# Attention operands padded to 128 rows of zeros, masks in fp32r of 256 columns, one transfer for both heads, and other banks and places for sums, loads and projection steps

## The chip, the cores and the metric

One core of one Trainium2 chip runs the whole kernel. The metric is the device time of an execution in microseconds; the time before is the median of three runs, 1707.32 us (1706.2 to 1708.44).

## The reference

One step of a hybrid layer on two sequences: a prompt of 1024 frames, and a sample of 64 new frames with 256 frames of cache. Each layer normalises the input, makes one combined projection, feeds a part of its columns to RWKV-7 heads and a part to attention heads with a forget bias, projects both results back, and ends in a SwiGLU feed-forward. The part that the change touches is the attention with the output projection behind it (8 heads of 64):

```python
def _fox_attend(q, k, v, lc_q, lc_k, pos_q, pos_k):
    s = jnp.einsum('bqhd,bshd->bhqs', q, k, preferred_element_type=jnp.float32) * (HEAD_DIM ** -0.5)
    decay_bias = jnp.transpose(lc_q, (0, 2, 1))[..., :, None] - jnp.transpose(lc_k, (0, 2, 1))[..., None, :]
    causal = pos_k[None, :] <= pos_q[:, None]
    p = jax.nn.softmax(jnp.where(causal, s + decay_bias, -jnp.inf), axis=-1)
    return jnp.einsum('bhqs,bshd->bqhd', p.astype(v.dtype), v)
...
    mix = jnp.concatenate([y_rwkv, y_fox], axis=-1) @ w_out
    x = x + gt1[:, None] * mix
    h2 = _rms_norm(x, norm2_g) * (1 + sc2[:, None]) + sh2[:, None]
    ffn = (jax.nn.silu(h2 @ w_ffn_gate) * (h2 @ w_ffn_up)) @ w_ffn_down
```

## The kernel before, in words

The 1088 tokens go in two halves: half 0 is the first 512 prompt tokens, half 1 the other 512 and the 64 of the sample. In the profiled execution the projections and the RWKV heads take about the first 660 us, with the first attention pair of half 0 among their end. From about 680 to 909 us runs the attention of the rest, together with the output projection of half 0; from there to 1702 us the output projection of half 1 and the feed-forward.

**Attention.** Heads go in pairs, four pairs for each half. Numbers are split into a high and a low part (both in fp32r, a format of TensorE), and a score is the sum of two matmuls into one bank of PSUM (`pst`): `ka` with `qa` (128 rows: high and low keys against the high queries twice) and `kb` with `qb`. `kb` and `qb` have 73 rows: 64 of high keys or low queries, five rows of ones against the row maxima, and four rows of the summed log-forget values. Before the scores, `att_max` makes a maximum of each query's scores from `kb` and `qc` alone (bank `pmx`, reduced by VectorE into `nmx`); `att_rows` transposes the maxima on TensorE (`pnm`) and VectorE writes them into the five rows of `qb`. `att_main` then runs over blocks of 128 keys: score, mask on the diagonal, exponential on ScalarE (`pt`), sum over blocks on VectorE and GpSimd (`acc`), and the product with the values two blocks later (`pav`). A pair ends with the column sums over `acc` (`psm`), their inverse by Ln and Exp on ScalarE, and the scaled result `fy`. In half 1, the 64 sample queries have their own scores and values (`pss`, `pvs`).

**Masks** are matmuls too: the identity times `cmask`, 128 columns of bf16, added to the bank of the diagonal block.

**Loads.** The operands lie in DRAM as `qx` and `kx`, 132 rows for each head. `pair_load` fetches them, in parts: 0 is `qc` and `kb`, 1 is `qb`, `qa` and `ka`, 2 the values. Each head has its own tiles and transfers, 8 in part 0 and 10 in part 1. All are issued by SyncE (SP) in program order, beside the stores.

**Order.** The Tile scheduler orders the first part. In `att_second` the order of TensorE is that of the program (`te.on`): the four pairs of half 1 ("big" pairs) are walked block by block, and at each of 25 yields of a big pair one step is taken of `low`, the generator of pairs 1 to 3 of half 0 ("low" pairs). When these have ended, `load_mix` fetches the mixed rows, and two blocks later `proj_steps` begins, the output projection of half 0 (`po`, 64 steps of three matmuls), with three steps at a block. The low pairs keep their operands in rows of the buffers of the mix (`mixrh`, `mixrl`, `mixfh`, `mixfl`) and their `pt` and `acc` in the residual buffer (`x_0`).

**Banks.** `pmx` has two banks ("mx"), which it shares with `pnm`, `psm`, `pss` and `pvs`; `pst` has three ("st"), and the low pairs' `pav` and `po` lie in "mm".

Of the kernel before, what the change touches and what calls it, by code (L numbers as in the profile page):

```python
# [64 lines left out]
class K:  # L65
# [631 lines left out]
    def ones_rows(self):  # L697
        nc = self.nc

        cones = self.slot([2, 448], F32R, name="cones")  # L700
        nc.vector.tensor_copy(cones, self.ones[0:2, 0:1].to_broadcast([2, 448]))
        for scr, r, n, w in ((self.qx, 130, SP + SS, 272), (self.kx, 128, SP + PAST + SS, 448)):
            for i in range(0, n, w):
                nc.sync.dma_start(scr[:, r:r + 2, i:i + w].rearrange("h r t -> r h t"),
                                  cones.bitcast(F32)[:, 0:w].unsqueeze(1).to_broadcast([2, 8, w]))

    def logf(self, hf):
# [70 lines left out]
        for g in (order[0:4], order[4:]):  # L778
            if not g:
                continue  # L780
            g = sorted(g, key=lambda e: e[2])
            if g[0][2] != hf.t0:
                pr = self.ps([32, 4, P], tag="fx", name="plr")
                rows = self.slot([32, 4, P], F32R, name="lrow", tag="fx")
            ck = g[0][2]
            prf, rf = pr.rearrange("r x t -> r (x t)"), rows.rearrange("r x t -> r (x t)")
            for i, _, c, m, _ in g:
                nc.tensor.transpose(prf[:, c - ck:c - ck + m], q4[0:m, i].rearrange("p a h -> p (a h)"),
                                    self.ident[0:m, 0:m])
            w = sum(m for _, _, _, m, _ in g)  # L790
            nc.vector.tensor_copy(rf[:, 0:w], prf[:, 0:w])
            cq = g[0][4]
            wq = sum(m for _, _, _, m, c in g if c is not None)
            for part in range(2):
                r = 16 + 8 * part
                nc.sync.dma_start(self.kx[:, 130 + part, ck:ck + w], rf[r:r + 8, 0:w].bitcast(F32))
                nc.sync.dma_start(self.qx[:, 128 + part, cq:cq + wq], rf[8 * part:8 * part + 8, 0:wq].bitcast(F32))
# [38 lines left out]
    def put_split(self, src, j, t0, n, is_k):  # L836

        nc = self.nc
        hi = self.slot([P, 576], F32R, name="shi", tag="fx")
        lo = src.bitcast(F32R)  # L840
        self.split(hi[:, 0:n], lo, src, pool_lo=self.pool_lo)
        for x, r in ((hi, 0 if is_k else 64), (lo, 64 if is_k else 0)):
            for h in range(2):
                t = (self.kx if is_k else self.qx)[2 * j + h, r:r + 64]
                nc.sync.dma_start(t[:, t0:t0 + n], x[64 * h:64 * h + 64, 0:n].bitcast(F32))
# [24 lines left out]
    def att_consts(self, ap):  # L870
        nc = self.nc
        self.identb = ap.tile([P, P], BF16, name="identb")
        nc.vector.tensor_copy(self.identb, self.ident)
        self.cmask = []
        for x in range(2):
            cm = self.slot([P, P], name="cm")
            nc.gpsimd.memset(cm, 0.0)
            nc.gpsimd.affine_select(out=cm, in_=cm, compare_op=ALU.is_ge, fill=NEG, base=0,
                                    pattern=[[2 * x - 1, P]], channel_multiplier=1 - 2 * x)
            self.cmask.append(ap.tile([P, P], BF16, name=f"cmask{x}"))  # L880
            nc.vector.tensor_copy(self.cmask[x], cm)
# [4 lines left out]
    def ones_keys(self, kb):  # L886
        self.nc.gpsimd.tensor_copy(kb[64:69], self.ones[64:69, 0:1].to_broadcast([5, kb.shape[1]]))

    def no_rows(self, qc):
        self.nc.gpsimd.memset(qc[64:69].bitcast(F32), 0.0)  # L890

    def pair_ops(self, pool):

        nq, nk = 640, SP + PAST + SS
        t = {n: pool.tile(s, F32 if n == "v" else F32R, name=n)
             for n, s in (("kb2", [73, nk]), ("kb3", [73, nk]), ("v", [P, 11, P]), ("qb0", [73, nq]), ("qb1", [73, nq]),
                          ("qa0", [P, 576]), ("qa1", [P, 576]), ("ka0", [P, nk]), ("ka1", [P, nk]),
                          ("kb0", [73, nk]), ("kb1", [73, nk]), ("qc0", [73, nq]), ("qc1", [73, nq]))}
        self.pops = {n: [t[f"{n}{i}"] for i in range(4 if n == "kb" else 2)] for n in ("kb", "qc", "ka", "qa", "qb")}
        self.pops["v"] = t["v"]  # L900
        for t in self.pops["kb"]:
            self.ones_keys(t)
        for t in self.pops["qc"]:
            self.no_rows(t)
            self.nc.gpsimd.memset(t[:, 576:640].bitcast(F32), 0.0)

    def pair_bufs(self, g, big):
# [3 lines left out]
        g["tags"] = {"st": "st", "mx": "mx", "pv": "pv" if big else "mm", "sm": "mx"}  # L911
        return g

    def pair_get(self, j):

        g = {n: [t[(2 * j + h) % len(t)] for h in range(2)] for n, t in self.pops.items() if n != "v"}
        g["v"] = self.pops["v"]
        return self.pair_bufs(g, True)

    def pair_first(self, pool):  # L920

        g = {n: [pool.tile([r, 512], F32R, name=f"{n}f{h}") for h in range(2)]
             for n, r in (("kb", 73), ("qc", 73), ("ka", P), ("qa", P), ("qb", 73))}
        for h in range(2):
            self.ones_keys(g["kb"][h])
            self.no_rows(g["qc"][h])
        return self.pair_bufs(g, True)

    def pairs_low(self):

        (m0, m1), (l0, l1) = self.mixhi, self.mixlo
        a, b, c, d, e, f = [[t[:, k, 0:512] for k in range(4)] for t in (m0.a, l0.a, m1.a, l1.a, m0.b, l0.b)]
        one = {"kb": a[0:2], "qc": a[2:4], "ka": b[0:2], "qa": b[2:4], "qb": c[0:2]}
        two = {"kb": c[2:4], "qc": d[0:2], "ka": d[2:4], "qa": [e[2], f[2]], "qb": [e[3], f[3]]}
# [6 lines left out]
        for j in (1, 2, 3):  # L941
            g = out[j]
            for k in ("kb", "qc", "qb"):
                g[k] = [t[0:73] for t in g[k]]
            if j < 3:
                for h in range(2):
                    self.ones_keys(g["kb"][h])
                    self.no_rows(g["qc"][h])
# [5 lines left out]
    def pair_load(self, j, hf, g, part):  # L954
# [5 lines left out]
        for h in range(2):  # L960
            hd = 2 * j + h
            ka, kb, qa, qb, qc = [g[x][h] for x in ("ka", "kb", "qa", "qb", "qc")]
            if part == 0:
                ld(qc[0:64, 0:n], self.qx[hd, 64:128, q])
                ld(qc[69:73, 0:n], self.qx[hd, 128:132, q])
                ld(kb[0:64, 0:NK], self.kx[hd, 0:64, 0:NK])
                ld(kb[69:73, 0:NK], self.kx[hd, 128:132, 0:NK])
            elif part == 1:
                ld(qb[0:64, 0:n], self.qx[hd, 0:64, q])
                ld(qb[69:73, 0:n], self.qx[hd, 128:132, q])  # L970
                for r in (0, 64):
                    ld(qa[r:r + 64, 0:n], self.qx[hd, 64:128, q])
                ld(ka[:, 0:NK], self.kx[hd, 0:128, 0:NK])
# [9 lines left out]
    def att_max(self, j, hf, g):  # L983
# [4 lines left out]
        for h in range(2):  # L988
            pc = self.tpool.tile([P, 4, 2], F32, tag="pc", name="pc") if hf.smp else None
            for t in range(5 if hf.smp else 4):  # L990
                smp = t == 4
                qn, nk, k0 = (SS, 320, SP) if smp else (P, hf.t0 + (t + 1) * P, 0)
                for x, c in enumerate(range(0, nk, 512)):
# [5 lines left out]
                    if c + m == nk:  # L999
                        d = 0 if smp else m - qn  # L1000
                        te.matmul(ps[0:qn, d:d + qn], self.identb[0:qn, 0:qn], self.cmask[0][0:qn, 0:qn], start=False,
                                  stop=True, skip_group_check=True)
# [6 lines left out]
    def att_rows(self, j, hf, g):  # L1009
# [5 lines left out]
        for h in range(2):  # L1015
            r = slice(32 * h, 32 * h + 5)
            nc.vector.tensor_tensor(g["qb"][h][64:69, 0:nt * P].rearrange("p (t q) -> p t q", q=P),
# [3 lines left out]
    def att_main(self, j, hf, g):  # L1021
# [11 lines left out]
        def scores(b, c0):  # L1033
            r = []
            for h in two:
# [6 lines left out]
                if diag:  # L1042
                    te.matmul(ps[:, c0:c0 + P], self.identb, self.cmask[1], start=False, stop=True, skip_group_check=True)
# [42 lines left out]
        if hf.smp:  # L1086
            ps = self.ps([P, 2, 3, SS], tag=tags["sm"], name="pss")
            for h in two:
# [4 lines left out]
                te.matmul(ps[0:SS, h, 2], self.identb[0:SS, 0:SS], self.cmask[1][0:SS, 0:SS], start=False, stop=True,  # L1093
# [28 lines left out]
        pd = self.ps([P, 512], tag=tags["sm"], name="psm")  # L1122
# [33 lines left out]
    def proj_steps(self, hf):  # L1156

        w = [self.load_w(self.A["w_out"][0], [P, KT, P])]
        for o in range(KT):
# [5 lines left out]
            for k in range(KT):  # L1165
                for y, (l, r) in enumerate(((wh, mh), (wh, ml), (wl, mh))):
                    self.te.matmul(ps[:, 0:hf.n], l[:, k], r[:, k, 0:hf.n], start=(k == 0 and y == 0),
                                   stop=(k == KT - 1 and y == 2))
                if k == KT - 1:
# [3 lines left out]
    def att_second(self, hf, h0, g, low):  # L1173
# [3 lines left out]
        po, mix, start = iter(()), iter(()), 0  # L1177
        for j in range(4):
# [4 lines left out]
            for b in self.att_main(j, hf, g):  # L1183
                if low and next(low, 1) == 1:
                    low, mix = None, self.load_mix(h0)
                    fill(mix, 2)
                    self.residual_x(h0)
                    start = 8 * j + (b if isinstance(b, int) else 7) + 2
                if b == "v":
                    if nxt:  # L1190
# [3 lines left out]
                        fill(po, 2)  # L1194
                        self.att_rows(j + 1, hf, nxt)
                    fill(po, 2)
                elif b in ("h", "b"):
                    fill(mx, 1)
                    fill(mix, 1)
                else:  # L1200
                    if start and 8 * j + b == start:
                        po = self.proj_steps(h0)
                    fill(po, 3)
                    fill(mx, b % 2)
                if b == 7 and nxt:
                    fill(mx, 99)
                    self.pair_load(j + 1, hf, nxt, 1)
                    fill(po, 1)
            fill(po, 1)
# [7 lines left out]
    def load_mix(self, hf):  # L1217
# [3 lines left out]
        for m in range(4 if hf.smp else 5):  # L1221
# [361 lines left out]
    def run(self):  # L1583
        tc, nc, A, O = self.tc, self.nc, self.A, self.O
        halves = [Half(0), Half(1)]
        with ExitStack() as top:
# [8 lines left out]
            self.qx = D1("qx", [8, 132, SP + SS])  # L1595
# [117 lines left out]
            mix1, x1s, attp, mix0 = [top.enter_context(ExitStack()) for _ in range(4)]  # L1713
# [4 lines left out]
            self.pair_ops(L(attp, "attp"))  # L1718
# [5 lines left out]
            gs = self.pairs_low()  # L1724
            g = self.pair_get(0)
# [16 lines left out]
            attp.close()  # L1742
# [214 lines left out]
```

## Time and profile before

| | |
|---|---|
| median of three runs | 1707.32 us |
| profiled execution | 1703.8 us, its span 1702.1 us |
| instructions | 31944, of them 12783 matmuls |
| TensorE busy | 1635.9 us, 96% of the span |
| TensorE idle | 66.2 us (the span less its busy time) |
| mean granted clock of TensorE | 0.969 of full speed |
| VectorE, ScalarE, GpSimd busy | 1050.2, 660.6 and 180.0 us |
| DMA | 200.18 MB, mean 118 GB/s |

The profiled execution's time is its span and 1.7 us around it, and it lies 3.5 us under the median of the runs. A matmul's busy time has its length at the clock that was granted: at a clock of 0.50 TensorE can be busy all the time and do half the work. So the table's 96% has to be read with the granted clock of the stage beside it.

### The profile page before, as it was taken

To read this page: it belongs to the slowest core of one execution; us is meant where nothing else is said; L and a number is where in the kernel's file an instruction comes from. 1 tells how busy PE (TensorE), PEld (TensorE's weight loads), DVE (VectorE), ACT (ScalarE), POOL (GpSimd) and SP (SyncE) were. 2 spreads that over 40 slices of the span, in tenths; PEclk is the share of its full clock that TensorE was granted. 3 is DMA by queue.
4 is the path that set the end of the run, shared out by engine and by line. 5 is a ranking of instruction groups with operands and counts; after the bars stand their busy time and mean duration, and the time that the engine had idled before them with its cause. 6 is when DMAs were issued, how large, how long until landed. Compare 5 with 4: busy or idle time off the path is not lost.

```text
span 1702.1 us, 31944 instructions
## 1 busy us (share of the span) xinstructions
PE 1635.9 (96%) x12783; PEld 1400.2 (82%) x12783; DVE 1050.2 (62%) x2162; ACT 660.6 (39%) x1284; POOL 180.0 (11%) x314
## 2 busy tenths in 40 slices
PE   6999999999999998699999999999999999999999
PEld 3767767788878886455668999999999999999998
DVE  6677676758767635454556985555555555545545
ACT  4544465745454354033335643333333333112210
POOL 1101101120202204132341000000000000000000
PEclk8999999999999999587999999999999999999999
DMA  8544466512233344824644433222222215423313
GB/s 308 162 112 119 140 190 201 157 52 64 58 96 79 95 126 122 211 72 115 187 146 152 152 116 103 80 77 76 77 77 77 76 65 161 154 94 96 96 38 124
DMA packets 130019, 200.18 MB, mean 118 GB/s; under 512 B 61838, under 2 KB 68526, under 8 KB 129870
## 3 DMA queue, kind: packets, MB, share of 16 engines
q1 hardware_dynamic: 129870, 198.14, 38.5%
q8 instruction: 100, 1.64, 0.4%
q14 instruction: 49, 0.40, 0.1%
HBM read 154.90 MB, written 43.19 MB: 116 GB/s over the span
## 4 chain that ended last, share of the span: by engine, by line
PE 78%; DVE 8%; ACT 4%; DMA 4%; issue 2%; SPq 2%; POOL 0%; DVEq 0%; ACTq 0%; POOLq 0%
PE pd L1515 15%; PE pfe L1400 8%; PE pfc L1400 8%; PE pfa L1400 7%; PE pmm L323 4%; PE pmm L325 4%; PE pmm L324 4%; PE pfb L1400 4%; PE pst L1860 3%; PE pbs L404 2%; PE po L1860 2%; PE pav L1860 2%; PE pmx L1860 1%; PE pS L662 1%; SPq L958 1%
## 5 line engine op out<-in xcount | busy, mean ns | idle before, releaser
L323 PE MATMUL pmm<-hhi,whi 128*128 128x288 f32 (+1 forms) x624 | 218.0, 350 | 2.4 <-ACT pb L346 2.4
L324 PE MATMUL pmm<-hlo,whi 128*128 128x288 f32 (+1 forms) x624 | 216.0, 346 | 0.2 <-DVE hlo L301 0.2
L325 PE MATMUL pmm<-hhi,wlo 128*128 128x288 f32 (+1 forms) x624 | 213.1, 342 | 0.0
L241 ACT CAST whi<-wraw 128x1024 fp32r<-128x1024 f32 (+2 forms) x116 | 99.2, 855 | 222.8 <-PE pd L1515 163.4
L1515 PE MATMUL pd<-al,whi 128*128 128x512 f32 (+1 forms) x528 | 172.4, 327 | 0.0
L1515 PE MATMUL pd<-ah,whi 128*128 128x512 f32 (+1 forms) x528 | 172.2, 326 | 0.0
L1515 PE MATMUL pd<-ah,wlo 128*128 128x512 f32 (+1 forms) x528 | 172.2, 326 | 0.0
L1519 DVE SCALAR_TENSOR_TENSOR x1t<-pd,mod,x1t 128x512 f32<-128x512 f32 x192 | 91.1, 498 | 106.8 <-PE pd L1515 106.2
L323 PEld LDWEIGHTS pmm<-hhi,whi 128*128 128x128 f32 x624 | 118.6, 190 | 17.8 <-issue 3.7
L324 PEld LDWEIGHTS pmm<-hlo,whi 128*128 128x128 f32 x624 | 118.5, 190 | 11.2 <-issue 1.7
L325 PEld LDWEIGHTS pmm<-hhi,wlo 128*128 128x128 f32 x624 | 118.3, 190 | 10.9 <-issue 1.7
L245 DVE TENSOR_TENSOR wlo<-wraw,whi 128x1024 fp32r<-128x1024 f32 (+2 forms) x108 | 104.7, 970 | 28.0 <-ACT whi L241 27.7
L1515 PEld LDWEIGHTS pd<-ah,whi 128*128 128x128 f32 x528 | 99.1, 188 | 7.1
L1515 PEld LDWEIGHTS pd<-ah,wlo 128*128 128x128 f32 x528 | 99.1, 188 | 7.1
L1515 PEld LDWEIGHTS pd<-al,whi 128*128 128x128 f32 x528 | 99.1, 188 | 7.0
L1400 PE MATMUL pfc<-hh,hS 128*128 128x256 f32 (+1 forms) x352 | 102.3, 291 | 1.1 <-ACT hh L1302 1.1
L1400 PE MATMUL pfc<-hh,lS 128*128 128x256 f32 (+1 forms) x352 | 102.4, 291 | 0.0
L1400 PE MATMUL pfa<-hh,whi 128*128 128x256 f32 (+1 forms) x352 | 102.1, 290 | 0.0
L1400 PE MATMUL pfa<-hl,whi 128*128 128x256 f32 (+1 forms) x352 | 101.8, 289 | 0.0
L1400 PE MATMUL pfa<-hh,wlo 128*128 128x256 f32 (+1 forms) x352 | 101.6, 289 | 0.0
L1400 PE MATMUL pfc<-hl,hS 128*128 128x256 f32 (+1 forms) x352 | 101.3, 288 | 0.0
L1347 ACT CAST hS<-wraw 128x512 fp32r<-128x512 f32 x88 | 53.6, 619 | 62.3 <-PE pfc L1400 61.4
(437 smaller groups left out, 4106.4 us busy)
## 6 DMA issues: line engine op xcount, KB each, us to landing
wraw<-in_w_in_dram SPq DMA_DIRECT2D x52, 512.0 KB
wada<-in_w_ada_dram SPq DMA_DIRECT2D x48, 512.0 KB
as<-actscr SPq DMA_DIRECT2D x22, 544.0 KB
wraw<-in_w_gate_dram SPq DMA_DIRECT2D x22, 512.0 KB
wraw<-in_w_up_dram SPq DMA_DIRECT2D x22, 512.0 KB
wraw<-in_w_down_dram SPq DMA_DIRECT2D x40, 256.0 KB
wraw<-in_w_out_dram SPq DMA_DIRECT2D x16, 512.0 KB
actscr<-sg SPq DMA_DIRECT2D x22, 288.0 KB
```

The source lines that it names most:

```text
L241: nc.scalar.copy(hi, src)
L245: eng.tensor_tensor(lo, src, hi.bitcast(F32), op=ALU.subtract)
L323: nc.tensor.matmul(ps[0:M, 0:n], whi[:, k, 0:M], xhi[:, k, off:off + n], start=(k == 0), stop=False)
L324: nc.tensor.matmul(ps[0:M, 0:n], whi[:, k, 0:M], xlo[:, k, off:off + n], start=False, stop=False)
L325: nc.tensor.matmul(ps[0:M, 0:n], wlo[:, k, 0:M], xhi[:, k, off:off + n], start=False, stop=(k == kt - 1))
L404: nc.tensor.matmul(ps[:, 0:n], w, x[:, off:off + n], start=True, stop=True)
L662: nc.tensor.matmul(ps, kb[:, c], sv[:, c], start=True, stop=True)
L1347: nc.scalar.copy(w[x][0], src)
L1400: nc.tensor.matmul(ps, l[:, k], r[:, s, k], start=(first and k == 0 and y == 0), stop=(k == 3 and y == 2), skip_group_check=True)
L1515: nc.tensor.matmul(ps[:, 0:n], w[:, i], x[:, t:t + n], start=(i == 0 and y == 0), stop=(i == len(fs) - 1 and y == 2))
L1519: nc.vector.scalar_tensor_tensor(dst, ps[:, so - off:so - off + l], self.mod[:, 40 + o, b:b + 1], dst, op0=ALU.mult, op1=ALU.add)
L1860: return self.pin(self.tc.nc.tensor.matmul(*a, **k))
```

## The change

The change has these parts.

1. **Rows.** All tiles of `kb`, `qc` and `qb` get 128 rows. GpSimd clears rows 64 to 127 and writes the ones at 96 to 100 (`aux_rows`); the four log-forget rows move from 69 to 64. The matmuls of these operands then have 128 rows instead of 73.
2. **Masks.** The identity and `cmask` are fp32r, and a mask has 256 columns, of which 128 are zeros (64 columns at the sample's scores).
3. **Transfers.** A tile holds both heads, `[128, 2, n]`, and one transfer fills it: part 0 has 2 transfers, part 1 has 4, in the order `qa`, `qa`, `ka`, `qb`. `qx` gets 136 rows and `kx` another order, so that the 68 rows of an operand lie together; writing the log-forget rows of `qx` takes four more transfers for the ones.
4. **Buffers.** `kb` of the big pairs is double (`kb0`, `kb1`), all else single. `pair_ops` stands behind `pairs_low`, so its clearing follows that of the low pairs.
5. **Banks.** `psm` has a tag of its own, "dn": banks of "st" for the big pairs; the low pairs' `psm`, `pnm` lie in "mm".
6. **Steps beside the big pairs.** `side()` takes 30 low steps for a big pair instead of 25 (four at "v"), and the projection's steps begin as soon as the low pairs have ended, with 2 or 3 at a block.
7. **Rows of the mix.** The projection adds rows 4 to 7 first; `load_mix` begins with row 4, and this one is fetched at the start of the second half.

The core of the diff:

```diff
     def att_consts(self, ap):
...
-            self.cmask.append(ap.tile([P, P], BF16, name=f"cmask{x}"))
-            nc.vector.tensor_copy(self.cmask[x], cm)
+            self.cmask.append(ap.tile([P, 3 * P], F32R, name=f"cmask{x}"))
+            nc.gpsimd.memset(self.cmask[x].bitcast(F32), 0.0)
+            nc.vector.tensor_copy(self.cmask[x][:, P:2 * P], cm)
...
-    def ones_keys(self, kb):
-        self.nc.gpsimd.tensor_copy(kb[64:69], self.ones[64:69, 0:1].to_broadcast([5, kb.shape[1]]))
-
-    def no_rows(self, qc):
-        self.nc.gpsimd.memset(qc[64:69].bitcast(F32), 0.0)
+    def aux_rows(self, kb, *rest):
+        nc = self.nc
+        for t in (kb, *rest):
+            nc.gpsimd.memset(t[64:128].bitcast(F32), 0.0)
+        nc.gpsimd.tensor_copy(kb[96:101], self.ones[96:101, 0:1].unsqueeze(2).to_broadcast([5, *kb.shape[1:]]))
...
+        t = {n: pool.tile([P, *s], F32 if n == "v" else F32R, name=n)
+             for n, s in (("kb1", [2, nk]), ("v", [11, P]), ("qb", [2, nq]), ("qa", [2, 576]), ("ka", [2, nk]),
+                          ("kb0", [2, nk]), ("qc", [2, nq]))}
+        self.pops = t
+        self.aux_rows(t["kb0"], t["qc"], t["qb"])
+        self.aux_rows(t["kb1"])
...
-        g["tags"] = {"st": "st", "mx": "mx", "pv": "pv" if big else "mm", "sm": "mx"}
+        g["tags"] = {"st": "st", "mx": "mx"} | ({"pv": "pv", "sm": "mx", "dn": "st"} if big else
+                                                {"pv": "mm", "sm": "mm", "dn": "mm"})
...
-            if part == 0:
-                ld(qc[0:64, 0:n], self.qx[hd, 64:128, q])
-                ld(qc[69:73, 0:n], self.qx[hd, 128:132, q])
-                ld(kb[0:64, 0:NK], self.kx[hd, 0:64, 0:NK])
-                ld(kb[69:73, 0:NK], self.kx[hd, 128:132, 0:NK])
...
+        if part == 0:
+            ld(qc[0:68, :, 0:n], row(self.qx, 68, 136, q))
+            ld(kb[0:68, :, 0:NK], row(self.kx, 64, 132, slice(0, NK)))
+        elif part == 1:
+            for r in (0, 64):
+                ld(qa[r:r + 64, :, 0:n], row(self.qx, 68, 132, q))
+            ld(ka[:, :, 0:NK], row(self.kx, 0, 128, slice(0, NK)))
+            ld(qb[0:68, :, 0:n], row(self.qx, 0, 68, q))
...
-                    te.matmul(ps[:, c0:c0 + P], self.identb, self.cmask[1], start=False, stop=True, skip_group_check=True)
+                    te.matmul(ps[:, w:w + 256], self.identr, self.cmask[1][:, P - c0 + w:P - c0 + w + 256], start=False,
+                              stop=True, skip_group_check=True)
...
-        pd = self.ps([P, 512], tag=tags["sm"], name="psm")
+        pd = self.ps([P, 512], tag=tags["dn"], name="psm")
...
+        mix, po = self.load_mix(h0), self.proj_steps(h0)
+        fill(mix, 1)
+        on = [True]
+
+        def side(n):
+            for _ in range(n):
+                if on and next(low, 1) == 1:
+                    on.clear()
+                    fill(mix, 2)
+                    self.residual_x(h0)
+                elif not on:
+                    fill(po, 1)
...
                 if b == "v":
...
-                        fill(po, 2)
+                        side(2)
                         self.att_rows(j + 1, hf, nxt)
-                    fill(po, 2)
+                    side(2)
...
-                    if start and 8 * j + b == start:
-                        po = self.proj_steps(h0)
-                    fill(po, 3)
+                    side(1 if on else 3 - (j == 1 or j == 2 and b % 2))
...
-        for m in range(4 if hf.smp else 5):
+        for m in (0, 1, 2, 3) if hf.smp else (4, 0, 1, 2, 3):
```

How the instructions stand after it, at three places. On SP, at the loads of the low pairs where the second half begins, before (`mixrh` and `mixrl` are the low pairs' tiles, `yscr` takes the last RWKV result `y` and the first pair's `fy`):

```order
L958 DMA mixrh_8303<-qx 64x512
L958 DMA mixrh_8303<-qx 4x512
L958 DMA mixrl_8305<-qx 64x512
L958 DMA mixrl_8305<-qx 4x512
L958 DMA mixrh_8303<-kx 64x512
L958 DMA mixrh_8303<-kx 4x512
L958 DMA mixrl_8305<-qx 64x512
L958 DMA mixrh_8343<-qx 64x512
L694 DMA yscr_72<-y 128x576
L958 DMA mixrh_8343<-qx 4x512
L958 DMA mixrh_8343<-kx 64x512
L958 DMA mixrh_8343<-kx 4x512
```

and after:

```order
L953 DMA mixrl_8294<-kx 128x2x512
L953 DMA mixrh_8292<-qx 68x2x512
L953 DMA mixrl_8294<-qx 68x2x512
L953 DMA mixrh_8292<-kx 68x2x512
L953 DMA mixrl_8312<-qx 64x2x512
L694 DMA yscr_72<-y 128x576
L953 DMA mixrh_8311<-qx 68x2x512
L953 DMA mixrh_8311<-kx 68x2x512
L1128 DMA yscr_71<-fy 128x512
L953 DMA qa<-qx 64x2x576
L953 DMA qc<-qx 68x2x576
L953 DMA kb_8326<-kx 68x2x1344
```

Five transfers of both heads now stand ahead of the store of `y`, where ten of one head did (the last eight are shown), four of them of four rows; and right behind the store of `fy` the loads of the first big pair begin.

On TensorE, at the change from the first big pair to the second, before:

```order
L1860 MATMUL pvs<-accs,ones 64x64 x2
L1863 MATMUL pnm<-ident,nmx_8138 64x128
L1860 MATMUL psm<-acc,ones 64x512 x2
L1860 MATMUL pss<-qa_8319,ka_8321 128x64
L1860 MATMUL pss<-qb_8317,kb_8314 128x64
```

and after:

```order
L1863 MATMUL pvs<-accs,ones 64x64 x2
L1863 MATMUL pav<-x_0_8299,v_8468 64x256 x2
L1863 MATMUL pav<-x_0_8299,v_8468 64x128 x2
L1866 MATMUL pnm<-ident,nmx_8125 64x128
L1863 MATMUL psm<-x_0_8299,ones 64x512 x2
L1863 MATMUL pst<-mixrl_8312 128x512
L1863 MATMUL pst<-mixrh_8292,mixrh_8311 128x512
L1863 MATMUL pst<-cmask_8121,identr 128x256
L1866 MATMUL pnm<-ident,nmx_8127 64x128
L1863 MATMUL pst<-mixrl_8312 128x512
L1863 MATMUL pst<-mixrh_8292,mixrh_8311 128x512
L1863 MATMUL pst<-cmask_8121,identr 128x256
```

Between the big pair's `pvs` and its `psm` now stand steps of low pairs: the end of one, with a `pnm` and a `psm` of its own right behind each other, and the first scores of the next.

On TensorE, the mask in the first maxima of a big pair, before (`kb_8323` and `qc_8325` are one head's operands):

```order
L1860 MATMUL pmx<-kb_8323,qc_8325 128x512
L1860 MATMUL pmx<-kb_8323,qc_8325 128x256
L1860 LDWEIGHTS identb
L1860 MATMUL pmx<-cmask_8126,identb 128x128
L1860 MATMUL pmx<-kb_8323,qc_8325 128x512
```

and after:

```order
L1863 MATMUL pmx<-kb_8326,qc 128x512
L1863 MATMUL pmx<-kb_8326,qc 128x256
L1863 MATMUL pmx<-cmask_8113,identr 128x256
L1863 MATMUL pmx<-kb_8326,qc 128x512
L1863 MATMUL pmx<-kb_8326,qc 128x384
```

The weight load that stood by itself ahead of a bf16 mask is gone, and the mask has twice the columns.

103 lines of the change are left out of this document (42 added, 61 removed).

## The prediction

> **What bounds the kernel now.** I read the page first: engines, then the granted clock in 40 slices.
>
> ```profile
> span 1702.1 us, 31944 instructions
> ...
> PE 1635.9 (96%) x12783; PEld 1400.2 (82%) x12783; DVE 1050.2 (62%) x2162; ACT 660.6 (39%) x1284; POOL 180.0 (11%) x314
> ...
> PEclk8999999999999999587999999999999999999999
> ```
>
> TensorE is busy throughout, and its clock falls in slices 17 to 19 alone, a stretch of some 130 us. So I asked for the stages by windows (busy time of PE, PEld, DVE, ACT, POOL, then granted clock, DMA share, GB/s), with the borders where the clock changes.
>
> ```profile
> 0.00:660.00 660.00, 627.21 (x5977) 498.91 (x5978) 440.15 (x1057) 341.89 (x721) 101.25 (x240) 0.99 0.45 130
> 682.50:719.50 37.00, 23.14 (x65) 14.34 (x65) 17.51 (x34) 1.69 (x3) 2.84 (x6) 0.50 0.84 217
> 719.50:737.00 17.50, 17.46 (x51) 11.10 (x53) 8.05 (x15) 5.26 (x10) 4.79 (x5) 0.50 0.31 67
> 737.00:743.80 6.80, 6.28 (x33) 3.58 (x30) 3.50 (x8) 1.53 (x4) 1.36 (x2) 1.00 0.21 60
> 743.80:747.20 3.40, 3.40 (x16) 1.86 (x16) 1.94 (x5) 0.60 (x1) 0.32 (x1) 0.50 0.66 196
> 747.20:771.10 23.90, 21.20 (x130) 11.56 (x129) 13.64 (x28) 7.84 (x18) 7.61 (x10) 1.00 0.46 128
> 771.10:795.00 23.90, 22.82 (x71) 13.63 (x72) 10.08 (x18) 10.54 (x20) 7.16 (x7) 0.50 0.32 75
> 829.10:835.90 6.80, 6.80 (x19) 5.19 (x19) 2.00 (x4) 1.70 (x4) 1.40 (x1) 0.50 0.82 249
> 908.60:1702.00 793.40, 787.29 (x5806) 762.36 (x5804) 482.93 (x885) 239.41 (x406) 1.44 (x1) 1.00 0.31 100
> ```
>
> The ends, 0 to 660 and 908.6 to 1702, are TensorE's own work at full clock; the change has nothing to win there. Between them the attention waits for loads until 719.5 (PE 23 of 37 us busy, DMA share 0.84), and then runs four stretches at half clock in which TensorE is busy nearly all the time. Three more views tell about these: PE alone in windows of 3.4 us (busy time, clock, DMA share, GB/s), a row of PE's timeline (start, length), and all engines while the loads run.
>
> ```profile
> 726.80:730.20 3.40, 3.40 (x13) 0.50 0.00 0
> 730.20:733.60 3.40, 3.40 (x12) 0.50 0.02 5
> 767.70:771.10 3.40, 1.57 (x11) 1.00 1.01 232
> ```
>
> ```profile
> 734.00 3.38 PE L1860 MATMUL pav<-pt,v 128*64 128x512 f32 x8
> ```
>
> ```profile
> 668.00:680.00 12.00, 10.13 (x55) 5.52 (x53) 8.13 (x17) 5.30 (x13) 5.02 (x9) 1.00 0.27 76
> 688.00:708.00 20.00, 14.60 (x38) 8.20 (x38) 14.30 (x27) 0.00 (x0) 0.00 (x0) 0.50 0.97 243
> ```
>
> The clock stayed at 0.50 over stretches in which TensorE had no gap, and came back at 737.0, when eight `pav` of all 128 rows had run. What stood before were scores, maxima and masks, of which the `kb` matmuls feed 73 of 128 rows. So busy time alone doesn't bring the clock back here; how much of the array is fed seems to count. From 688 to 708 the loads run at 243 GB/s with a share of 0.97; over the whole stage they reach 217, and before 680 only 76.
>
> **The change part by part,** against the profiled execution's 1703.8 us, which lies 3.5 us under the median.
>
> ```profile
> 679.06 0.35 SPq L694 DMA_DIRECT2D yscr<-y  x1
> ```
>
> *A, transfers.* 217 GB/s for 37 us are 8.0 MB; at 243 GB/s they take 33.0 us: 4.0 less. That time lies where the queue has gaps between its 18 transfers a pair, and I take it to go with 6. The store of `y`, which SP issues at 679.06 when it is ready (the row above), stands behind five transfers of both heads instead of ten of one: 1.62 MB (128+68+68+68+64 rows of 2x512 words) instead of 0.79 MB (six of 64 rows, four of 4) can move in the quiet 668 to 680 (0.27 share): 0.83 MB at 243 GB/s are 3.4 us more. Together −7 (0 if the queue is bound by more than issues; −9 if the first wait goes whole). PE's waits show that loads end last:
>
> ```profile
> PE pmx L1860 <- DMA mixrh<-qx: 6.8, 1, 6.8
> ...
> PE psm L1860 <- DVE qb L1017: 2.7, 3, 1.8
> ...
> PE pss L1860 <- DMA ka<-kx: 1.6, 2, 1.2
> ```
>
> *B to E, rows.* A matmul doesn't get longer by its rows, as the spacing shows: 0.23 us behind 128 rows, 0.23 behind 73.
>
> ```profile
> 891.79 0.39 PE L1860 MATMUL pst<-qa,ka 128*128 128x512 f32 x1
> 892.02 0.39 PE L1860 MATMUL pst<-qb,kb 73*128 73x512 f32 x1
> 892.25 0.23 PE L1860 MATMUL pst<-cmask,identb 128*128 128x128 bf16 x1
> 892.29 0.48 PE L1860 MATMUL pst<-qa,ka 128*128 128x512 f32 x1
> ```
>
> ```profile
> 877.10 0.28 PE L1860 MATMUL pss<-qa,ka 128*128 128x64 f32 x1
> 877.21 0.28 PE L1860 MATMUL pss<-qb,kb 73*128 73x64 f32 x1
> 877.41 0.21 PE L1860 MATMUL pss<-cmask,identb 64*64 64x64 bf16 x1
> 877.56 0.50 PE L1860 MATMUL pst<-qa,ka 128*128 128x512 f32 x1
> ```
>
> ```profile
> 1002.40 0.29 PE L1400 MATMUL pfc<-hh,hS 128*128 128x256 f32 x1
> 1002.52 0.28 PE L1400 MATMUL pfc<-hl,hS 128*128 128x256 f32 x1
> ```
>
> So padding costs TensorE nothing, and wins what the clock gives. I take it that rows of zeros count as fed, and that a full stream is then released after one to two of the 3.4 us steps, 5.1 us in the mean. The trace has no zero rows, so both ends stay: nothing, and never throttled.
> - B, 719.5 to 737.0: 17.5 us at half clock; 12.4 of them after release take 6.2 less. −6.2 (0 to −8.75).
> - C, 743.8 to 747.2: 3.4 us. −1.7 (0 to −1.7).
> - D, 771.1 to 795.0: 23.9 us. Never throttled −12, throttled at the same place and released after 5.1 us −9.4; mean −10.7 (0 to −12). It is throttled behind the pair's change at 767.7 to 771.1, where PE was busy for 1.57 of 3.40 us; term F shortens this gap.
> - E, 829.1 to 835.9, the same at the next pair: −3.4 or half of it, −2.5 (0 to −3.4).
>
> By the Trainium skill (the page "TensorE: Matmul & The Clock Gate", section "What's actually happening") the clock is released after about 3.4 us of sustained activity. By that rule alone the stream would have been released by 727 without a padded row, and padding would be worth nothing; the rows at 726.80 and 730.20, busy throughout at 0.50, disagree, so I keep B to E, and the rule's outcome is a rival below.
>
> *F, sums.* `psm` waited for `qb` (DVE) because `pnm` and both shared two banks: 2.7 us. In three banks of `st` this wait goes for the big pairs. In its place, the low pairs' `pnm` and `psm` stand right behind each other in "mm", and the rows of `qb` take VectorE this long:
>
> ```profile
> 768.25 1.65 DVE L1017 TENSOR_TENSOR qb<-pnm,ident 5x640 fp32r<-5x640 f32 x2 [1.06 <-PE pnm L1863]
> ```
>
> I put 2.5 us (one and a half such) against it: −0.2 (−2.7 to +2.2).
>
> *G, masks.* A bf16 mask takes 0.04 us and the matmul behind it starts 0.32 later instead of 0.23: 0.13 each. 256 columns in fp32r take 0.12 (1002.40 to 1002.52): 0.01 less, for 128 such masks by the code 1.3 us. Round the 8 masks of `pss` two starts lie 0.35 us apart (877.21 to 877.56); two plain matmuls of 64 columns take 2x0.11 (877.10 to 877.21 is one), so 0.13 each, 1.0 us. −2.3 together (−2.3 to +1: so small a difference as 0.01, times 128, can turn round).
>
> *H.* At full clock TensorE meets VectorE sooner: in 747.2 to 771.1 it idled 2.7 of 23.9 us. Some 15 us of B to E's work at that share: +1.6 (0 to +3).
>
> *I, both heads in one transfer.* The first `pss` needs one head of `ka` only, and now waits for two: 128x1344 words are 0.69 MB, 2.8 us at 243 GB/s, at three changes 8.5 at most. Low steps now stand between, and before only 1.6 us were waited in all: +1.4, half of one (0 to +8.5).
>
> *J, GpSimd.* Clearing is by columns:
>
> ```profile
> L887 POOL CAST kb<-ones 5x1344 fp32r<-5x1344 f32 x4 | 5.1, 1301 | 2.4 <-PE plora L397 2.4
> ...
> L890 POOL MEMSET qc<- 5x640 f32 x2 | 1.2, 626 | 0.0
> ```
>
> 0.98 ns a column: 2x2688+2x1280 columns cleared are 7.8 us and 2x2688 of ones 5.2, so 13.0 instead of 6.3. The first loads of `qc` and `kb` wait for it: from 678.6, where GpSimd's first such work begins when the RWKV part lets go of the space, `qc` is clear 3.9 us later (2688+1280 columns) and `kb0` has its ones at 686.4 (1280 and 2688 more). Ahead of `kb` SP issues two transfers of low pairs, `qa` and `qc` behind the store of `y`, 1.16 MB, which keep the DMA engines busy for 4.8 us at 243 GB/s, from about 681. So 0, and 6.7 if that cover is gone.
>
> *K.* Steps at "v", the order of the projection's rows, the earlier row 4 and four more transfers of ones within 0 to 660: all lie beside a busy TensorE (627 of 660 there): 0. The scheduler also reorders the first part: ±4.
>
> Sum: −7−6.2−1.7−10.7−2.5−0.2−2.3+1.6+1.4 = −27.6, so 1676.2 for the profiled execution and 1680 for the median (+3.5).
>
> **The rivals.**
> - *Rows of zeros don't count for the clock* (the array does no work with them). B, C, D, E and H fall away: −8.1, a median of 1699. No row of the trace has zero operands, so neither side has a direct witness; for the likeliest case speaks only that fully busy stretches differ by their rows. By the skill's rule above the time would be the same, as no stretch there would be shorter.
> - *Loading isn't shortened*, since a share of 0.97 means that the DMA engines were full; the stage ends at 719.5 as before. −20.6: 1687. For it: 243 GB/s over 20 us; against: 76 GB/s before 680.
> - *Slower: transfers of both heads come late at every pair's change.* All of part 1 (`qa` 0.59, `ka` 1.38, `qb` 0.31 MB) is 2.28 MB, 9.4 us at 243 GB/s, and can start only when both heads of the pair before were read. Waited for whole at three changes it costs 28.2 instead of I's 1.4, and a TensorE idle that long is throttled again, so D and E go too: −27.6+26.8+13.2 = +12.4, a median of 1720. It decides from 5.3 us at each change (−27.6+13.2−1.4 = −15.8 is what three such would eat up). For it: the DMA share at 767.7 to 771.1 is 1.01 already. Against: 1.6 us of waits in all.
> - *No net change*: the zeros don't count and the transfers cost what A wins, 1707.
>
> **How the numbers follow.** The likeliest case 0.58; zeros don't count 0.18; loading as before 0.14; slower 0.06; none 0.04. The likeliest's own range is 1670 to 1692 (A's and D's ends, ±4 of K). The range must hold 8 in 10 and so takes in 1699 with 3 of K's 4 us, and the low end with as much below the likeliest's: 1667 to 1702. A measurement of this kernel tells about 0.2%, 3.4 us: faster 0.90, same 0.04, slower 0.06.
>
> **What would show it.** B to E: a granted clock of 1.00 within some 7 us of the loads' end, and no half clock over 8 us behind it; if a busy stream of padded matmuls stays at 0.50, zeros don't count. A: the first `pmx` of the low pairs starts without a wait of 6.8 us, and the last loads land 7 us nearer to the end of the RWKV part. F: no wait of `psm` for DVE at big pairs. I: waits of `pss` for `ka` under 3 us in all. The prediction is wrong if these hold and TensorE then waits for VectorE or ScalarE in their place, or if the first 660 us move by more than 4.

## The result, and the profile after

The changed kernel takes 1782.86 us (median of four runs, 1782.63 to 1784.0) against 1707.88 us of the kernel before on the same chip: a ratio of 1.0441 (1.0423 to 1.0460). It is 75 us slower, where 27 us less were forecast. Three executions of the kernel before in later sessions were in a slower state (1719.8, 1788.5 and 2303.9 us) and stand in no ratio or median below. The page after, its head and the clock in 40 slices:

```profile
span 1781.1 us, 31815 instructions
...
PE 1646.1 (92%) x12783; PEld 1419.3 (80%) x12783; DVE 1047.4 (59%) x2162; ACT 660.6 (37%) x1284; POOL 185.0 (10%) x315
...
PEclk9998999999998999578888999999999999999999
```

TensorE has the same 12783 matmuls and 10 us more of busy time, but 135 us idle where it had 66. Two marks split the span: the last store of an RWKV result, `yscr<-y`, which SP issues when the first part ends, and the first `po` of half 1, where the attention stage has ended. Rows of the view by tile (duration min/median/max in ns, first and last start in us), before and after:

```profile
L694 SPq DMA_DIRECT2D yscr<-y x8: 320/332/585, 175.3 to 679.1; - x8
```

```profile
L694 SPq DMA_DIRECT2D yscr<-y x8: 326/338/577, 180.7 to 708.8; - x8
```

The attention stage runs from there to 908.6 before and to 987.7 after. So the first part is 29.7 us longer, the attention 278.9 us instead of 229.5, and the rest the same, 793.4 and 793.3 us (the last row below). Windows of the changed kernel, columns as in the prediction:

```profile
100.00:200.00 100.00, 91.56 (x872) 62.99 (x860) 64.56 (x183) 43.40 (x93) 11.59 (x28) 0.91 0.38 106
500.00:600.00 100.00, 94.68 (x871) 80.99 (x872) 60.83 (x134) 45.52 (x104) 8.82 (x22) 0.91 0.33 85
720.00:740.00 20.00, 7.42 (x20) 4.83 (x20) 5.95 (x12) 0.00 (x0) 3.51 (x3) 0.50 0.74 187
740.00:760.00 20.00, 15.76 (x42) 10.46 (x42) 11.68 (x24) 1.09 (x2) 0.00 (x0) 0.50 0.44 128
760.00:780.00 20.00, 8.11 (x35) 6.96 (x36) 5.05 (x10) 5.34 (x10) 2.42 (x4) 0.62 0.25 81
820.00:840.00 20.00, 9.92 (x37) 7.80 (x34) 4.70 (x10) 6.49 (x14) 3.96 (x4) 0.58 0.32 111
880.00:900.00 20.00, 4.59 (x17) 3.80 (x18) 0.80 (x3) 2.04 (x5) 2.26 (x2) 0.53 0.60 170
940.00:960.00 20.00, 11.29 (x38) 8.33 (x37) 3.15 (x7) 4.84 (x9) 3.77 (x2) 0.66 0.54 160
987.70:1781.00 793.30, 787.41 (x5806) 762.30 (x5804) 482.87 (x885) 239.28 (x406) 1.43 (x1) 1.00 0.30 100
```

TensorE is idle for nearly half of the time or more at the start of the second half (720 to 740, 760 to 780) and at each change of a big pair (820, 880 and 940), with the clock falling each time. In the first part it is idle more too, at a lower clock, in the first two windows above. The same windows of the kernel before:

```profile
100.00:200.00 100.00, 98.46 (x1035) 71.26 (x1027) 70.47 (x190) 48.69 (x103) 16.60 (x35) 1.00 0.48 128
500.00:600.00 100.00, 97.60 (x999) 84.77 (x999) 65.87 (x159) 49.01 (x117) 17.59 (x31) 1.00 0.34 90
```

The waits of PE in the changed kernel say what it waits for in the attention:

```profile
PE pmx L1863 <- DMA kb<-kx: 22.9, 2, 12.9
PE pss L1863 <- DMA qb<-qx: 15.8, 3, 6.1
PE pmx L1863 <- DMA mixrh<-kx: 11.6, 1, 11.6
PE pss L1863 <- DMA ka<-kx: 10.8, 3, 5.8
PE pmx L1863 <- DMA v<-vtok: 5.9, 1, 5.9
```

67 us of waits for loads in all. Yet the DMA engines are far from full while it waits. Single transfers stand in the chain of waits (issue, length to landing) for times that their bytes can't explain at the 243 GB/s of the prediction: 731 KB of `kb` stand for 24.67 and 18.72 us, 313 KB of `qb` for 14.75 and 14.43. These lengths hold the wait behind earlier transfers too.

```profile
713.75 24.67 DMA kb<-kx
753.03 18.72 DMA kb<-kx
...
812.89 14.75 DMA qb<-qx
...
881.17 18.63 DMA v<-vtok
...
937.05 14.43 DMA qb<-qx
```

The 18.63 us of `v` belong to 32 KB, the last piece of the values: 64 rows of the sample, issued at 881.17. By the packets of the trace (512 bytes each) 48 of these rows had moved by 884.3; the last 16 moved from 897.9 to 900.9, behind the packets of a `kb` that had been issued 10 us earlier. `pmx`, which the view puts behind `v` here, doesn't read the values; it reads this `kb`, whose last packet landed at 899.2.

The stretch of the second `kb`, in windows of 4 us, and one within the first `qb`, shows the cause's mark: a DMA share of 0.25 or 0.26, a quarter of 16 engines, and no more.

```profile
764.00:768.00 4.00, 0.00 (x0) 0.00 (x0) 0.00 (x0) 0.00 (x0) 0.00 (x0) 0.50 0.26 82
768.00:772.00 4.00, 0.12 (x1) 0.14 (x1) 0.00 (x0) 0.00 (x0) 0.00 (x0) 0.50 0.25 77
824.00:828.00 4.00, 0.31 (x2) 0.31 (x2) 0.65 (x2) 1.15 (x3) 1.40 (x1) 0.50 0.26 88
```

### The profile page after: what moved, and what is told of

Same layout as the page of the kernel before. It is cut to its first block, busy times and chain, and to the rows that moved or that the text cites. A ratio compares the mean times of both kernels' runs of the same rounds, so it can differ in the third digit from the quotient of the medians.

```text
span 1781.1 us, 31815 instructions
## 1 busy us (share of the span) xinstructions
PE 1646.1 (92%) x12783; PEld 1419.3 (80%) x12783; DVE 1047.4 (59%) x2162; ACT 660.6 (37%) x1284; POOL 185.0 (10%) x315
## 4 chain that ended last, share of the span: by engine, by line
PE 77%; DVE 8%; DMA 7%; ACT 4%; issue 3%; POOL 0%; SPq 0%; POOLq 0%; DVEq 0%; ACTq 0%
PE pd L1517 15%; PE pfc L1402 7%; PE pfe L1402 7%; PE pfa L1402 7%; PE pmm L323 5%; PE pmm L325 5%; PE pmm L324 5%; PE pfb L1402 4%; DMA kb<-kx 2%; PE po L1863 2%; PE pbs L404 2%; PE pst L1863 2%; DMA qb<-qx 2%; PE pmx L1863 2%; PE pav L1863 2%
```

## The experiments

Two theories stood first. ROWS: the new transfers have 68 rows, and such a transfer keeps only 4 of the 16 DMA engines busy. BOTH: a transfer that fills both heads' tile starts and lands too late. ORDER is about the first part, ZEROS about the clock. The times of the runs come from later sessions, on three chips, on which the kernel before has a median of 1704 to 1707 us with a wider scatter (1693 to 1718); so ratios to it are what counts. The attention's length is that of one profiled execution each, between the two marks above; only one kernel was profiled twice (once64, again in probe): 234.0 and 234.3.

| kernel | median us | ratio to before, 95% interval | attention us |
|---|---|---|---|
| before (first session) | 1707.88 | 1 | 229.5 |
| changed (first session) | 1782.86 | 1.0441 (1.0423 to 1.0460) | 278.9 |
| split64 | 1732.58 | 1.0165 (1.0133 to 1.0198) | 232.4 |
| heads68 | 1749.92 | 1.0267 (1.0212 to 1.0322) | 245.4 |
| once64 | 1715.58 | 1.0062 (1.0031 to 1.0092) | 234.0 |
| heads64 | 1704.14 | 1.0003 (0.9976 to 1.0030) | 224.3 |
| heads64steps | 1709.23 | 1.0014 (0.9985 to 1.0042) | 224.8 |
| headfirst | 1699.78 | 0.9971 (0.9940 to 1.0002) | 218.6 |
| beforepad | 1696.89 | 0.9946 (0.9921 to 0.9970) | 212.2 |
| padmask | 1699.64 | 0.9973 (0.9946 to 1.0000) | 220.7 |
| padbank | 1696.76 | 0.9963 (0.9933 to 0.9992) | 214.6 |
| padmaskbank | 1699.60 | 0.9956 (0.9936 to 0.9976) | 219.8 |

**split64.** Rows 64 to 67 get a transfer of their own:

```diff
-            ld(kb[0:68, :, 0:NK], row(self.kx, 64, 132, slice(0, NK)))
+            for a, b in ((0, 64), (64, 68)):
+                ld(kb[a:b, :, 0:NK], row(self.kx, 64 + a, 64 + b, slice(0, NK)))
```

and `qc`, `qb` in the same way.

> The changed kernel with each transfer of 68 rows (both heads) cut into one of 64 and one of 4 rows; all else as changed. Theory ROWS (a transfer of 68 rows keeps only 4 of the 16 DMA engines busy, as the DMA share of 0.25 from 764 to 772 us says): the loads run at 200 GB/s and more again, the attention falls from 279 us back to 230 or less, median 1705 to 1735. Theory BOTH (loads are late because one transfer and one tile hold both heads, so that it starts later and all must land): that is untouched, median 1775 to 1785. The first part stays 30 us longer under either.

1732.58 us: 2.8% of the 4.4% are gone with nothing but a cut at row 64, and the attention is back at 232.4 us. More transfers, faster: ROWS holds.

**heads68.** The 68 rows stay, but each head has its transfer: `ld(kb[0:68, h, 0:NK], self.kx[2 * j + h, 64:132, 0:NK])`, and so for the others.

> The changed kernel with a transfer for each head, still of 68 rows; tiles, rows, masks, banks and order as changed. ROWS: each of them still keeps 4 engines busy, median 1770 to 1790. BOTH: the first head's operands land earlier, a third or more of the 49 us in the attention comes back, median below 1767.

1749.92 us, lower than ROWS alone gave it. Its waits of PE:

```profile
PE pmx L1865 <- DMA kb<-kx: 19.8, 3, 12.1
PE pmx L1865 <- DMA mixrh<-kx: 9.1, 1, 9.1
PE pss L1865 <- DMA qb<-qx: 6.6, 4, 2.1
```

Those for `kb` stay; those for `qb` fall from 15.8 to 6.6, those for `ka` (10.8) are no longer among the first. The attention is 245.4 us: cutting by heads brings back 33 of the 49 us though all 68 rows stay, where the cut at row 64 brought back 46. So the two causes can't be added up. My reading, not tested by itself, is that a slow transfer costs twice where TensorE waits for both heads of it. BOTH is part of the 49 us, though not the root. The two expectations were each half wrong, since I had set the theories against each other.

**probe.** The transfer by itself, at the end of once64: one tile, two heads, 2048 bytes for a row and head. The first of the thirteen still run beside the kernel's last work; the last eight stand alone.

```diff
+            probe = self.ring.tile([P, 2, 512], F32, tag="wraw", name="probe")
+            for r in (64, 64, 65, 68, 68, 72, 80, 96, 120, 127, 128, 68, 64):
+                nc.sync.dma_start(probe[0:r], self.kx[0:2, 0:r, 0:512].rearrange("h r t -> r h t"))
```

> once64 with thirteen transfers at its end that nothing needs, each of r rows x 2 heads x 2048 bytes into one tile, one after the other, r = 64, 64, 65, 68, 68, 72, 80, 96, 120, 127, 128, 68, 64. ROWS: a transfer is dealt to as many engines as divide its rows: 64, 80, 96 and 128 rows use 16 (128 rows, 0.5 MB, land in 2 to 3 us of movement), 68 rows use 4 (some 4 us of it for 0.28 MB, DMA share 0.25), 72 use 8 or 12, 120 use 15 or 8, and 65 and 127 rows 13 or 1. If the rate is the same for all r, ROWS is wrong and something else held the 68-row transfers.

Windows of the last eight, from the first packet to the last, of 72, 80, 96, 120, 127, 128, 68 and 64 rows (the last two columns are the DMA share and GB/s):

```profile
1721.83:1723.39 1.56, 0.00 (x0) 0.00 (x0) 0.00 (x0) 0.00 (x0) 0.00 (x0) 0.50 0.61 184
1725.12:1726.93 1.81, 0.00 (x0) 0.00 (x0) 0.00 (x0) 0.00 (x0) 0.00 (x0) 0.50 0.64 174
1728.30:1730.17 1.87, 0.00 (x0) 0.00 (x0) 0.00 (x0) 0.00 (x0) 0.00 (x0) 0.50 0.73 205
1731.65:1734.41 2.76, 0.00 (x0) 0.00 (x0) 0.00 (x0) 0.00 (x0) 0.00 (x0) 0.50 0.71 174
1735.96:1757.43 21.47, 0.00 (x0) 0.00 (x0) 0.00 (x0) 0.00 (x0) 0.00 (x0) 0.50 0.06 24
1758.92:1761.08 2.16, 0.00 (x0) 0.00 (x0) 0.00 (x0) 0.00 (x0) 0.00 (x0) 0.50 0.83 239
1762.38:1766.05 3.67, 0.00 (x0) 0.00 (x0) 0.00 (x0) 0.00 (x0) 0.00 (x0) 0.50 0.21 74
1767.86:1769.22 1.36, 0.00 (x0) 0.00 (x0) 0.00 (x0) 0.00 (x0) 0.00 (x0) 0.50 0.65 187
```

64 rows take 1.36 us, 68 rows 3.67 us at a share of 0.21, and 127 rows 21.47 us at 0.06, one engine of 16; 128 rows take 2.16. The share of 72 rows, 0.61, is over what 8 engines could give. The share by itself doesn't tell 12 engines from 16. But with each transfer the trace also has packets of 4 bytes: in the order of the windows 12, 16, 16, 15, 1, 16, 4 and 16 of them. The numbers fit a rule: the largest number up to 16 that divides the rows is the number of engines. The Trainium skill has this rule (the page "DMA: Bandwidth & Descriptors", section "Why a DMA increments its semaphore by 16 and not by 1": the largest k up to 16 that divides the slowest dimension on both sides). The trace agrees with it, by the 4-byte packets: 4 for 68 rows, 12 for 72, 15 for 120, 1 for 127.

**once64.** The log-forget rows and ones are written to `qx` once, in 132 rows, and read twice:

```diff
-        for scr, r, n, w in ((self.qx, 66, SP + SS, 272), (self.qx, 134, SP + SS, 272), (self.kx, 128, SP + PAST + SS, 448)):
+        for scr, r, n, w in ((self.qx, 66, SP + SS, 272), (self.kx, 128, SP + PAST + SS, 448)):
...
-                nc.sync.dma_start(self.qx.rearrange("h (c r) t -> h c r t", c=2)[:, :, 64 + part, cq:cq + wq],
-                                  rf[8 * part:8 * part + 8, 0:wq].bitcast(F32).unsqueeze(1).to_broadcast([8, 2, wq]))
+                nc.sync.dma_start(self.qx[:, 64 + part, cq:cq + wq], rf[8 * part:8 * part + 8, 0:wq].bitcast(F32))
```

> split64 with the log-forget rows and ones written to qx once (132 rows, no four more transfers of ones, no broadcast); TensorE's order in the first part is then that of the kernel before, row for row. Theory ORDER (the first part is 30 us longer because these writes change the order that the scheduler makes): the store of y comes at 679 us again, 30 us less than split64, median 1675 to 1705. If instead the work itself (clearing on GpSimd, larger masks) holds up the first part, its end stays near 709.

1715.58 us, 17 less than split64 on the same chip, with TensorE's order in the first part as before (the first 5985 matmuls of the trace). The last stores of `y`, of split64 and of once64:

```profile
L694 SPq DMA_DIRECT2D yscr<-y x8: 326/338/577, 180.2 to 705.9; - x8
```

```profile
L694 SPq DMA_DIRECT2D yscr<-y x8: 319/332/576, 178.4 to 688.9; - x8
```

17.0 us lie ahead of the attention, which is no shorter (234.0 against 232.4). ORDER holds in kind; it is 17 us instead of 30, and so 1715 instead of 1705 at most. Both numbers hang on single executions. Ten profiled executions, of before and of the other runs, have TensorE's first part in the order of before, and this store at 679.1 to 688.9: before's is the earliest of them, once64's the latest. The three with the new order (changed, split64, heads68) have it at 705.9 to 709.5. So the new order comes with 17 to 30 us.

**heads64.** once64 with each transfer cut by heads as well:

```diff
-        ld = lambda d, s: nc.sync.dma_start(d.bitcast(F32), s)
+        def ld(d, s):
+            for h in range(2):
+                nc.sync.dma_start(d[:, h].bitcast(F32), s[:, h])
```

> once64 with each transfer cut once more, one for each head (64 and 4 rows), in the same place and order. BOTH (what is left of the loss, 234 us of attention against 212 in beforepad, comes from transfers that land for both heads together): a half or more of the 22 us comes back, attention below 224 us, 10 us under once64. STEPS (it comes from the order of the program: 30 low steps a pair, buffers, when loads are issued): unchanged, attention 230 to 238.

0.6% less than once64, some 10 us, with intervals that just don't meet; attention 224.3. So landing together costs about 10 us even at full rate: nearly half of the 22, as BOTH had it, and short of the "half or more".

**heads64steps.** The function `att_second` of the kernel before, put into heads64.

> heads64 with the walk over the big pairs as in the kernel before (25 low steps a pair, the projection two blocks after their end at three steps a block, row 4 of the mix fetched after the low pairs). STEPS (what heads64 still loses against beforepad, 224 us of attention against 212, lies in this walk): attention below 219, median 5 to 10 us under heads64. If it lies in the masks, the banks and the throttle's chance: within 4 us of heads64, attention 221 to 227.

1.0014 against 1.0003, attention 224.8: the number of low steps at a big pair, the start of the projection and its two or three steps a block make no difference that shows. STEPS falls.

**headfirst.** heads64 with the loop over the heads outside that over the operands.

> heads64 with its loads issued head by head (all operands of a part for the first head, then for the second) as in the kernel before, instead of operand by operand for both heads. ORDER OF LOADS (what heads64 still loses against padmaskbank, 0.5%, is that the second head's rows stand ahead of what the first needs): ratio to before 0.994 to 0.998. If it lies in the tiles and buffers or elsewhere: 0.999 to 1.003, as heads64 and heads64steps.

0.9971 and 218.6 us lie where ORDER OF LOADS put them, but the intervals of headfirst and heads64 overlap (0.9940 to 1.0002, 0.9976 to 1.0030). It speaks for the theory and doesn't settle it.

**beforepad.** The kernel before with tiles of 128 rows, rows 64 to 127 cleared ahead of the ones and the loads, `qb` too:

```diff
     def ones_keys(self, kb):
+        self.nc.gpsimd.memset(kb[64:128].bitcast(F32), 0.0)
         self.nc.gpsimd.tensor_copy(kb[64:69], self.ones[64:69, 0:1].to_broadcast([5, kb.shape[1]]))
...
-        self.nc.gpsimd.memset(qc[64:69].bitcast(F32), 0.0)
+        self.nc.gpsimd.memset(qc[64:128].bitcast(F32), 0.0)
```

> The kernel before with operands of 128 rows, 73 to 127 zeros, and nothing else. ZEROS COUNT (the clock is granted by rows fed, zeros or not): the stretches at half clock from 720 us on shrink to some 5 us each, median 1683 to 1692. ZEROS DO NOT COUNT: the clock falls and comes back at the same places, median 1705 to 1710.

0.9946, a gain of 9 us by the ratio (5 to 13), between the two expectations. The profile says which mechanism it is; it is that of the fastest of the eight executions (1691.26 us). Windows of beforepad, cut where the clock changes:

```profile
689.90:727.40 37.50, 24.91 (x71) 15.73 (x72) 17.81 (x35) 2.88 (x5) 7.94 (x13) 0.51 0.86 231
727.40:768.30 40.90, 36.36 (x212) 21.17 (x211) 26.18 (x52) 13.78 (x31) 13.81 (x16) 0.99 0.35 102
768.30:778.60 10.30, 9.08 (x32) 5.34 (x32) 3.35 (x7) 3.47 (x7) 1.41 (x1) 0.54 0.90 212
778.60:897.70 119.10, 115.35 (x599) 74.57 (x598) 66.52 (x99) 49.55 (x92) 48.93 (x36) 1.00 0.46 142
```

In the kernel before, the stretches at half clock behind 682.5 added up to 88.6 us (37.0, 17.5, 3.4, 23.9 and 6.8); here they are 47.8 (37.5 and 10.3). The first, while the loads run, is as long as before; the clock now comes back with the loads' end, falls once at a pair's change, for 10 us instead of 24, and not again. All 12783 matmuls stand in the order of before. The attention as a whole, of before, beforepad, padmask, padbank and padmaskbank (the last three, below, have padded rows too; the granted clock is the third number from the end):

```profile
679.10:908.60 229.50, 205.62 (x926) 128.20 (x920) 113.29 (x193) 71.67 (x137) 69.91 (x63) 0.81 0.50 142
685.50:897.70 212.20, 187.60 (x926) 117.65 (x922) 114.99 (x193) 70.91 (x137) 76.49 (x69) 0.89 0.53 153
680.40:901.10 220.70, 193.41 (x925) 131.10 (x921) 115.28 (x193) 71.28 (x137) 75.24 (x69) 0.87 0.52 147
684.00:898.60 214.60, 186.86 (x925) 117.74 (x921) 114.19 (x193) 71.08 (x137) 76.43 (x69) 0.89 0.52 151
685.60:905.40 219.80, 191.01 (x925) 129.80 (x921) 114.82 (x194) 71.06 (x137) 75.72 (x69) 0.87 0.51 148
```

It is higher in each that is padded. So it is over all executions: the mean granted clock of a whole run has a median of 0.977 in the eight of beforepad (0.974 to 0.980) and of 0.970 in the 14 of before beside them (0.964 to 0.975). Rows of zeros count.

**padmask, padbank, padmaskbank.** beforepad with the masks, with the banks, with both, as in the diff of the change.

> beforepad with the masks of the change (fp32r, 256 columns, 64 at the sample). By the prediction's term G 2.3 us less than beforepad; if the wider masks queue, 1 us more. Median within 5 us of beforepad.

> beforepad with the banks of the change (psm of big pairs in the three banks of st, sums and rows of low pairs in mm). By the prediction's term F the waits of psm for qb go (2.7 us) and about as much comes at the low pairs: within 3 us of beforepad. If sums in st take banks from the scores, TensorE waits more in pst: some us longer.

> beforepad with both the masks and the banks of the change, the version put together from its parts that cost nothing in transfers. If padding is what wins and masks and banks are worth nothing: ratio to before 0.994 to 0.998 as for beforepad, padmask and padbank. If masks (2.3 us by term G) and banks help together: 0.991 to 0.994.

The intervals of all three overlap with that of beforepad: no gain of masks or banks shows. A mask does cost what was worked out, as PE's timeline of padmask shows (0.12 us from its start to the next):

```profile
740.48 0.28 PE L1869 MATMUL pst<-cmask,identr 128*128 128x256 f32 x1
740.60 0.34 PE L1869 MATMUL pmx<-mixrh,mixrl 128*128 128x384 f32 x1
```

The attention is 220 us in the two kernels with the new masks, 212 and 215 in the two without; whether the masks cost these 5 to 8 us, single executions don't settle. The wait of `pss` for `ka`, 5.0 us in padmask against 1.6 in beforepad, doesn't explain it, for padbank has 5.8. Of everything that ran, beforepad has the lowest ratio, and it beats both kernels; padmaskbank, the version put together, isn't better.

## Why the prediction was wrong

- **A, transfers, failed, and carries most of the miss.** The step that failed is "at 243 GB/s": I priced every new transfer by its bytes at a rate that the trace shows for transfers of 64 and 128 rows. The trace before holds no transfer of 68 rows, and I didn't bound this price below. It ran at 74 to 88 GB/s, on 4 of 16 engines; in place of −7 it cost 46 us (278.9 to 232.4 in the attention by one cut at row 64), with both heads in a transfer as here. A slip beside it: the ten transfers of one head are 0.82 MB with their four-row ones, not 0.79, which changes the sum by 0.1 us.
- **K, the first part, failed.** "±4" was a guess without a row. With four transfers of ones and the broadcast rows, TensorE's order is another from its 596th matmul on (93 us), and 2948 of the first 5985 stand in another place; the first part came out 17 to 30 us longer. In the windows above the loss shows as idle time and a clock of 0.91 in two stretches of 100 us where before it had been 1.00. That the first 660 us move by more than 4 was among the prediction's own signs of being wrong. Why this order is worse than the other stays open; that it comes with these writes is shown, that the order alone does it isn't.
- **B to E, the clock, right in kind.** Padding alone took the attention from 229.5 to 212.2 us, 17.3 less, where B to E and H forecast 21.1−1.6 = 19.5. In the other padded versions of before it is 9 to 15 us, and by the ratio over all executions some 9: the first part of beforepad ended at 685.5 us in the profiled execution, with its order unchanged, against 679.1 before, so single executions differ there by as much as is at stake.
- **I, both heads in one transfer, mis-sized.** +1.4, with 8.5 as the end; landing together at full rate measured about 10 us (once64 against heads64).
- **F and G, sums and masks:** −0.2 and −2.3 were forecast, and nothing beyond the intervals was found. In padbank the wait of `psm` for `qb` (2.7 us) is indeed gone, and the mask's 0.12 is as read; neither shows in the total.
- **J, GpSimd, right, but its close sum wasn't tested.** In the changed kernel `kb` was clear at 710.7, ahead of its load, which SP issued at 713.75, and had its ones at 718.5; the load landed 20 us later. The ones are hidden by a slow transfer, so whether the loads that I named would have covered them stays open.
- **The rivals.** "Slower: transfers of both heads come late at every pair's change" named the place and the sign, with a chance of 0.06 and 12 us. Its price was again bytes at 243 GB/s; `qb` alone stood for 14.75 and 14.43 us at two changes, from issue to landing. "Zeros don't count" is refuted by beforepad. The Trainium skill's rule (the page "TensorE: Matmul & The Clock Gate", section "What's actually happening": about 3.4 us of sustained activity release the clock) disagrees with that run too: padding, which adds no busy time, changed when it was released.

From one kernel to the other, by single profiled executions: 29.7 us in the first part, and in the attention −17.3 for padding, +46.5 for 68 rows and some 20 for the rest (212.2 to 232.4, of which heads landing together are about 10 and the order of loads perhaps 6); together 79, the difference of the spans. The signs and the largest term are sure; the single terms aren't, as the first part's 29.7 may be 17, padded versions of one kernel differ by 8 in the attention, and 33 of the 46.5 also come back when the heads are cut instead of the rows.

## What to carry to other kernels

Look at a transfer's row count before its bytes: cut it so that nearly all rows lie in a transfer whose rows are a multiple of 16 (64 and 4, not 68), and read a DMA share that stands at a quarter or a sixteenth as engines that were given nothing. Fewer transfers aren't cheaper if the first user must then wait for all that they bring. After an edit that only adds a few early transfers, compare the order of the whole program, since a scheduler may move everything behind them.

## What the runs showed of the hardware

- One transfer alone, 2 x 2048 bytes a row: 128 rows 239 GB/s, 64 rows 187, 68 rows 74, 127 rows 24.
- A transfer of 64 rows that was issued behind such a one waits for it with a part of its rows: of 32 KB of values, three quarters had moved 3 us after the issue, the last quarter 17 to 20 us after it.
- The 4-byte packets that the trace has with a transfer number 16 for 64, 80, 96 and 128 rows, 15 for 120, 12 for 72, 4 for 68 and 1 for 127.
- Rows of zeros count for the granted clock: padding operands from 73 to 128 rows, which costs a matmul no time (0.23 us from one of 512 columns to the next, with 73 rows and with 128), cut the time at half clock in the attention from 88.6 to 47.8 us in one profiled execution each; the mean clock of a whole run rose from 0.970 to 0.977 in the medians.
